# A two-layer decoder trunk on one core: latent attention driven by one list of steps, with stacked rotary queries, and FFN transposes moved into the next unit

## The chip, the cores and the metric

The kernel runs on one core of one Trainium2 chip. The metric is the device time of one execution, in microseconds, and what is compared is the median of several runs. An execution is a little longer than the span of its profile, which goes from the first to the last instruction.

The engines go by the names of the profile: PE is TensorE's matmuls and PEld its weight loads, DVE is VectorE, ACT is ScalarE, POOL is GpSimd, SP is SyncE, which issues the DMAs.

## The reference

The input is 256 tokens of width 1024 in float32. Two layers follow each other. Each layer has four sublayers, and behind each stands a layer norm of `ALPHA * x + delta`:

- a first FFN, half of `silu(x Wgate) * (x Wup)` times `Wout`, with an inner width of 2816;
- a mixer: forgetting attention (16 heads of 64) in layer 0, latent attention in layer 1;
- a second FFN of the same form;
- a projection of the layer's own input embedding, times a sigmoid gate of `x`.

The mixer that the change touches is the latent attention. From the stream that leaves layer 0 come, once, a compressed key/value of 256 columns (with an RMS norm) and one rotary key of 64 columns that all heads share. From the stream in layer 1 come compressed queries of 384 columns (with an RMS norm), and from these, per head, a query part of 128 columns without position and one of 64 columns that is rotated by position. The score of head h is

```
s = (q_nope . k_nope + rope(q_rope) . k_rope) / sqrt(192),   causal, then softmax
o = softmax(s) V,   V of 128 columns per head;   mix = concat(o) W_o
```

with 16 heads, and the rotation is `rope(x) = [x1 cos - x2 sin, x2 cos + x1 sin]` on the two halves of the 64 columns.

## The kernel before

**Precision by parts.** Every float32 operand of a matmul is kept as two parts: a high part, which a copy on ScalarE rounds to the format that TensorE takes at full rate, and a low part, the difference, which VectorE subtracts. A product is then three matmuls, high by high, high by low and low by high (`mm3`, L481). `parts` (L496) makes the two parts of something that TensorE has left in PSUM; weights are split the same way when they have landed (`Stream.split`, L149: the copy is L169, the subtraction L170).

**Tiles.** Tokens lie in two row blocks of 128. PSUM has eight banks, which are handed out from three rings (`bank`, L413): `y` with four, `h` with two, `tr` with two.

**The FFN** (`ffn`, L581) goes through eleven column chunks. The first two are computed with tokens as rows (`H`), so that their gated products must be transposed (`T`, L639, four transposes of 128 by 128). The other nine are computed transposed at once (`HT`, L651: 4 weight units of 24 matmuls, 256 columns wide), in three groups of three; the ring of a unit is `h` or `tr` by the chunk's number. Behind each group come the output products (`W`, L672, 512 columns wide). `T(0)` stands ahead of the first group and `T(1)` ahead of the second; ahead of the third stand the transposes of the compressed key/value, of the layer's input, or four idle ones. `ple_project` (L753) multiplies the layer's input behind the third group and takes four banks from `h`.

**The latent attention** (`mla`, L1217) is written out by hand. `dq` gives the compressed queries of one row block and normalizes them, `V` the values of four heads, `q_rope` the rotary queries of all 16 heads for one row block, `rope` (L1274) their rotation for eight heads: three multiplications and an addition, the addition of the first eight heads on GpSimd, the rest on VectorE. `transposed` turns the rotated queries, two heads to a transpose, and makes their two parts. Then the heads run through a pipeline: `gen(h + 1)` makes a head's keys and queries, `T(h - 1)` transposes the softmax weights of the head before, `QK(h)` makes the scores, `softmax(h)` (L1326) takes the row maxima (VectorE), the exponentials with their sums (ScalarE), the reciprocal (VectorE) and the division (GpSimd, L1344), `O(h - 2)` multiplies a finished head by its rows of the output weights, `AV(h - 1)` multiplies weights by values. `QK` (L1310) makes twelve matmuls a head: three for the part without position, three for the rotary part, each for a query block of 128 keys and one of 256. The rotary key of a pair of heads is kept twice, with zeros in the other head's half.

**What sets the order.** Each engine takes its instructions in the order in which the program issues them. Weights are loaded by SP into three raw buffers and split into ten slots (and a few lent tiles). When a split is issued is decided by a planner in `Stream`: it keeps estimates of when each engine is done, and `pump` (L242), called behind every `mm3`, splits the next unit if it has landed and the engines are free enough by the estimate. `hold` switches the pump off. `fill(n)` (L135) splits until n units are ready ahead, whatever the estimate. `ahead` (L128) issues only the high half, and `later` (L144) the low half. A unit that isn't ready when it is used is split at that point.

Of the kernel before, what the change touches and what calls it, by code (L numbers as in the profile page):

```python
# [30 lines left out]
LATE = 6  # L31
HAT = 12
FINE = 4
HOLD_MLA = True
AHEAD = {0: 4, 1: 4, 2: 4, 8: 4, 10: 4}
# [5 lines left out]
SW_DQ = 3  # L41
# [9 lines left out]
VT = {5: (2, (1,)), 8: (3, (0,)), 10: (3, (1,))}  # L51
# [345 lines left out]
class Trunk:  # L397
# [183 lines left out]
    def ffn(self, li, which, lni, kv=False, ple=False, at=None, cold=False):  # L581
# [57 lines left out]
        def T(c, ring="tr"):  # L639
# [59 lines left out]
        T(0)  # L699
        n = NCH  # L700
        late = [0, 2, 3, 4, 1] + list(range(5, n - STAG))
        for i, group in enumerate(GROUPS):
            if i == 1:
                T(1, "h")
            if i == 2:
                if kv:
                    self.kv_transpose()
                elif ple:
                    self.ple_transpose()
                else:  # L710
                    spare = self.bank("tr")
                    for k in range(4):
                        self.transpose(spare[:, 128 * k : 128 * k + 128], self.ident)
# [29 lines left out]
    def ple_transpose(self):  # L743
        nc = self.nc
        pt = self.ple_p
        tr = self.bank("tr")
# [6 lines left out]
    def ple_project(self, li):  # L753
# [3 lines left out]
        for t in range(2):  # L757
            for n in range(2):
                ps = self.bank("h")
# [434 lines left out]
    def kv_transpose_rope(self):  # L1194
# [3 lines left out]
        self.kr = [kvt[:, 1024 + 512 * s : 1536 + 512 * s].rearrange("p (i c) -> p i c", i=2) for s in range(2)]  # L1198
        b = self.bank("h")
        for t in range(2):  # L1200
            self.transpose(b[:, 128 * t : 128 * t + 128], self.kvtok[:, t, 256:384])
        nc.gpsimd.memset(self.kr[0][64:128, :, :].bitcast(F32), 0.0)
        nc.gpsimd.memset(self.kr[1][0:64, :, :].bitcast(F32), 0.0)
        for s in range(2):
            r = slice(64 * s, 64 * s + 64)
            self.parts(self.kr[s][r, 0, :], self.kr[s][r, 1, :], b[r, 0:256])

    def kv_transpose(self):
        b = self.bank("tr")
# [7 lines left out]
    def mla(self, li):  # L1217
# [9 lines left out]
        tmps = self.own([128, 4, 512], F32, "otb")  # L1227
        qk = self.own([128, 2, 2, 512], F32R, "qk")

        def dq(t, at=None, what=None, sweeps=SW_DQ):  # L1230
            ps = self.bank("y")
            self.moving(ps[:, 0:QR], t, ("dq",), QR, at, what, sweeps)
            rs = self.rms_scale(ps[:, 0:QR], QR, cqtok[:, t, 384:768])
            nc.vector.scalar_tensor_tensor(
                cqtok[:, t, 0:QR], ps[:, 0:QR], rs, qn, op0=ALU.mult, op1=ALU.mult
            )

        def V(g, ts, ring="h"):
            for t in ts:
                w = self.use(("kvv", g))  # L1240
                ps = self.bank(ring)
                for k in range(2):
                    self.mm3(
                        ps, lambda i: self.ckv[:, i, 256 * k + 128 * t : 256 * k + 128 * t + 128],
                        lambda i: w[:, i, 512 * k : 512 * k + 512], k == 0, k == 1,
                    )
                o = self.tl([128, 2, 512], F32R, "g4", 5)
                self.parts(o[:, 0, :], o[:, 1, :], ps)
                v[t, g] = o
# [11 lines left out]
        def q_rope(t, at=None, what=None):  # L1261
            ps = [self.bank("y") for _ in range(2)]
            for k in range(3):
                if k == at:
                    what()
                w = self.use(("qr", k))
                for n in range(2):
                    self.mm3(
                        ps[n], lambda i: cqt[:, i, k, 128 * t : 128 * t + 128],
# [152 lines left out]
        for h in range(16):  # L1422
            if 1 <= h < 15:
                gen(h + 1)
# [118 lines left out]
```

## Time and profile before

| | us |
|---|---|
| median of 3 runs | 1095.27 |
| range of the runs | 1094.84 to 1095.33 |
| profiled execution, its own time | 1094.83 |
| its span | 1092.7 |
| TensorE busy (matmuls) | 1075.1 |
| VectorE busy | 711.6 |
| ScalarE busy | 540.7 |
| GpSimd busy | 77.7 |

The profile is of one execution. Its table of groups gives, for each source line, engine and operation, the tile written and the tiles read, the count, the busy time, the mean of one in ns, and the idle time of the engine just before, with what ended it. The chain is followed back from the last instruction to what released it, so that it tells which work set the end. In a timeline, times are microseconds from the start of the span, and a row can hold several like instructions (x6). Matmuls are pipelined: the duration of one is longer than its distance to the next, so rates are read from a row that holds many. Line numbers are those of the listing above; most matmuls have L489, the helper, and all transposes but a few L493.

The latent attention lies between about 718 and 868 us of the span. In the stretch before it is the first FFN of layer 1, behind it the second.

### The profile page before, as it was taken

Reading aid. Unit: us, or ns where it says so; the run is one execution under the profiler, and the core shown is the slowest. Engines: PE = TensorE matmul, PEld = TensorE weight load, DVE = VectorE, ACT = ScalarE, POOL = GpSimd, SP = SyncE. Lnnn points to the kernel's source line nnn. Section 1 sums busy time; section 2 is a strip of 40 time slices with the busy share of each in tenths; the row PEclk is TensorE's granted clock in tenths of the full one; section 3 lists DMA queues with packets and bytes.
Section 4 is the critical chain, followed back from the end, with each engine's and each line's share of the span. In section 5 each row is a group of like instructions: output and inputs, shape, how many; then the busy total and the mean of one; then the engine's idle time right before and its main releaser. Section 6 shows DMA issues by size and latency. Waiting matters only on the chain.

```text
span 1092.7 us, 17699 instructions
## 1 busy us (share of the span) xinstructions
PE 1075.1 (98%) x7186; PEld 977.3 (89%) x7186; DVE 711.6 (65%) x1013; ACT 540.7 (49%) x796; POOL 77.7 (7%) x128
## 2 busy tenths in 40 slices
PE   9999999999999999999999999999999899999997
PEld 6999999899889999988899999988999789898986
DVE  5665545888897545548965554498776886455566
ACT  5554433667646434444554443245655465444431
POOL 0000000222200000001320000011111000000000
PEclk9999999999999999999999999999999999999999
DMA  8886652653358756455578554344453668565502
GB/s 283 287 276 241 192 185 81 193 173 134 120 169 294 231 185 198 148 182 164 168 256 270 189 183 159 97 103 132 145 160 116 191 221 295 182 201 193 179 15 77
DMA packets 150820, 198.54 MB, mean 182 GB/s; under 512 B 11858, under 2 KB 129874, under 8 KB 150740
## 3 DMA queue, kind: packets, MB, share of 16 engines
q1 hardware_dynamic: 150740, 197.43, 55.8%
q8 instruction: 56, 0.92, 0.3%
q14 instruction: 24, 0.20, 0.0%
HBM read 196.35 MB, written 1.05 MB: 181 GB/s over the span
## 4 chain that ended last, share of the span: by engine, by line
PE 83%; DVE 9%; issue 3%; ACT 2%; POOL 1%; DMA 1%; DVEq 0%; ACTq 0%; POOLq 0%; SPq 0%
PE h L489 35%; PE y L489 28%; PE tr L489 18%; DVE hl L170 2%; PE tr L493 2%; DVE x L569 1%; DVE st L551 1%; DVE x L550 1%; ACT hl L169 1%; POOL rs L561 1%; DMA raw<-in_ffn_w_in_dram 1%; ACT P L1337 1%; PE y L467 0%; DVE tr L1333 0%; DVE PT L499 0%
## 5 line engine op out<-in xcount | busy, mean ns | idle before, releaser
L170 DVE TENSOR_TENSOR hl<-raw,hl 128x1024 fp32r<-128x1024 f32 (+3 forms) x287 | 333.1, 1180 | 164.2 <-ACT hl L169 162.8
L169 ACT ACTIVATE hl<-raw 128x1024 fp32r<-128x1024 f32 (+3 forms) x287 | 285.3, 1016 | 193.3 <-PE y L489 94.0
L489 PE MATMUL h<-xT,hl 128*128 128x256 f32 x2064 | 245.5, 279 | 0.1
L489 PEld LDWEIGHTS h<-xT,hl 128*128 128x128 f32 x2064 | 240.9, 188 | 1.3 <-DVE qk L499 0.3
L489 PE MATMUL y<-hl,g 128*128 128x512 f32 x780 | 180.9, 390 | 0.0
L489 PEld LDWEIGHTS y<-hl,g 128*128 128x128 f32 x780 | 145.7, 188 | 29.8
L489 PE MATMUL tr<-xT,hl 128*128 128x256 f32 x864 | 102.7, 278 | 0.0
L489 PEld LDWEIGHTS tr<-xT,hl 128*128 128x128 f32 x864 | 100.8, 188 | 0.0
L489 PE MATMUL h<-hl,xT 128*128 128x512 f32 (+2 forms) x396 | 91.6, 381 | 0.7 <-DVE xT L499 0.6
L489 PEld LDWEIGHTS h<-hl,xT 128*128 128x128 f32 x396 | 70.8, 188 | 15.9 <-DVE xT L499 1.2
L489 PE MATMUL y<-hl,xT 128*128 128x512 f32 (+3 forms) x360 | 65.0, 334 | 0.2 <-DVE xT L499 0.2
L489 PEld LDWEIGHTS y<-hl,xT 128*128 128x128 f32 x360 | 55.4, 188 | 6.6 <-DVE xT L499 0.8
L561 POOL TENSOR_TENSOR rs<-ve,mhalf 128x1 f32<-128x1 f32 x16 | 15.2, 950 | 526.8 <-DVE ve L560 526.8
L498 ACT ACTIVATE xT<-tr 128x512 fp32r<-128x512 f32 x34 | 19.2, 596 | 55.7 <-PE tr L493 55.7
L499 DVE TENSOR_TENSOR g<-P,g 128x512 fp32r<-128x512 f32 x36 | 24.9, 693 | 25.1 <-ACT g L498 25.1
L498 ACT ACTIVATE g<-P 128x512 fp32r<-128x512 f32 x36 | 22.8, 632 | 31.0 <-DVE P L666 31.0
L489 PE MATMUL y<-hl,ota 128*128 128x512 f32 x144 | 36.0, 393 | 0.0
L170 DVE TENSOR_TENSOR otb<-raw,otb 128x1024 fp32r<-128x1024 f32 (+1 forms) x20 | 24.0, 1202 | 14.4 <-ACT otb L169 14.4
L170 DVE TENSOR_TENSOR qk<-raw,qk 128x1024 fp32r<-128x1024 f32 x21 | 25.7, 1223 | 11.7 <-ACT qk L169 11.6
L489 PEld LDWEIGHTS y<-hl,ota 128*128 128x128 f32 x144 | 26.0, 188 | 4.9
L665 ACT ACTIVATE P<-h 128x512 f32<-128x512 f32 x20 | 12.0, 598 | 37.1 <-PE h L489 37.1
L499 DVE TENSOR_TENSOR xT<-tr,xT 128x512 fp32r<-128x512 f32 x34 | 22.1, 682 | 12.2 <-ACT xT L498 12.2
(241 smaller groups left out, 1391.4 us busy)
## 6 DMA issues: line engine op xcount, KB each, us to landing
raw<-in_ffn_w_in_dram SPq DMA_DIRECT2D x172, 512.0 KB, 5.0
raw<-in_ffn_w_out_dram SPq DMA_DIRECT2D x44, 1024.0 KB, 5.2
raw<-in_fox_w_in_dram SPq DMA_DIRECT2D x11, 1024.0 KB, 5.3
raw<-in_ple_w_gate_dram SPq DMA_DIRECT2D x8, 1024.0 KB, 5.1
raw<-in_mla_w_o_dram SPq DMA_DIRECT2D x8, 1024.0 KB, 4.9
gb<-in_ln_g_dram SPq DMA_DIRECT2D x8, 512.0 KB, 6.4
gb<-in_ln_b_dram SPq DMA_DIRECT2D x8, 512.0 KB, 7.5
raw<-in_fox_w_o_dram SPq DMA_DIRECT2D x4, 1024.0 KB, 4.9
```

What stands on the lines that cost most here:

```text
L169: nc.scalar.activation(hi[:, c], src[:, c], AF.Copy)
L170: nc.vector.tensor_tensor(lo[:, c], src[:, c], hi[:, c].bitcast(F32), op=ALU.subtract)
L489: self.nc.tensor.matmul(out, lhsT, rhs, start=start, stop=stop)
L493: self.nc.tensor.transpose(out, in_, self.ident)
L498: self.nc.scalar.activation(hi, src, AF.Copy)
L499: self.nc.vector.tensor_tensor(lo, src, hi.bitcast(F32), op=ALU.subtract)
L550: nc.vector.scalar_tensor_tensor(xs, xs, alpha, y, op0=ALU.mult, op1=ALU.add)
L551: nc.vector.bn_stats(st, xs)
L561: nc.gpsimd.tensor_tensor(rs, ve, self.mhalf, op=ALU.pow)
L569: nc.vector.scalar_tensor_tensor(xs, xs, rs if i else mv[:, 0:1], self.gb[:, i, c0:c1], op0=ALU.mult if i else ALU.subtract, op1=ALU.add i ...
L665: nc.scalar.activation(gt, ps[0], AF.Silu)
L1337: nc.scalar.activation(P[:, c0:c1], b[:, c0:c1], AF.Exp, bias=nm[:, q : q + 1], scale=-1.0, accum_out=su[:, q : q + 1],)
```

## The change

- The rotary part of the scores is stacked. The 64 rotated columns of a head take 128 rows of one tile: their high parts one half, their low parts the other. One matmul against the key's high part (the same in both halves) gives high by high and low by high; a second against the key's low part, with zeros under the queries' low half, gives high by low. A head has ten score matmuls.
- For heads 0 to 7 the parts are made behind the transpose (`zT_first`: two copies and two subtractions on half the rows each). For heads 8 to 15 they are made ahead of it, side by side (`z_split`), and transposed together, one transpose a head and row block (`zT_last`).
- The rotation of heads 8 to 15 is a copy on ScalarE and four operations on GpSimd, and the subtraction for their low parts is on GpSimd as well. The addition of heads 0 to 7 is on GpSimd for row block 0 and on VectorE for row block 1.
- The division is on VectorE, and is a step of its own. Both row maxima stand ahead of both exponentials.
- A value tile's high copy and low subtraction are steps of their own, and so are the norm's scale, the reciprocal norm and the pump's fills.
- All steps of the latent attention stand in one list, `ORDER`, which a loop runs. Both row blocks of the compressed queries take the same order of terms.
- In the FFN each of the three transposes stands behind the first weight unit of its group, with the rings exchanged; `ple_project` alternates between `h` and `tr`.

```diff
+ORDER = (
+    "dq 0 0", "dq 0 1", "dq 0 2", "dq 0 3", "dq 0 4", "dq 0 5", "f 2", "dq 0 6", "hold 1", "dq 0 7", "dq 0 8",
+    "dq 0 9", "dq 0 10", "dq 0 11", "rms 0", "V 0 0", "V 0 1", "XT 1 0", "dqs 0", "vlo 0 0", "vlo 0 1", "V 1 0",
+    "l", "XT 1 1", "f 3", "dq 1 0", "dq 1 1", "dq 1 2", "dq 1 3", "cqT 0", "dq 1 4", "f 3", "dq 1 5", "dq 1 6",
+    "dq 1 7", "dq 1 8", "dq 1 9", "dq 1 10", "dq 1 11", "qr 0 0", "rms 1", "dqs 1", "rope 0 0 1", "vlo 1 0",
+    "V 1 1", "cqT 1", "exp", "qr 0 1", "qr 1 0", "f 3", "rope 1 0 0", "zT 0", "gen 0", "gen 1", "zT 1", "f 3",
+    "qr 1 1", "QK 0", "sm 0", "f 1", "QK 1", "sm 1", "div 1", "div 0", "f 3", "rope 0 1 2", "f 2", "vlo 1 1",
+    "V 2 0", "gen 2", "T 0", "gen 3", "f 1", "AV 0", "vlo 2 0", "rope 1 1 2", "a", "T 1", "f 4", "zs 0", "f 3",
+    "f 4", "QK 2", "zs 1", "y", "a", "sm 2", "div 2", "O 0 0", "O 0 1", "f 1", "AV 1", "f 4", "gen 4", "T 2",
...
+    "div 15", "l", "O 13 0", "AV 14", "f 1", "O 7 1", "gb", "hold 0", "O 8 1", "hold 1", "T 15", "O 9 1",
+    "AV 15", "O 14 0", "hold 0", "f 5", "f 3", "O 15 0", "ln 0", "O 10 1", "O 11 1", "O 12 1", "O 13 1",
+    "O 14 1", "XT 0 0", "XT 0 1", "O 15 1", "ln 1",
+)
...
-        def HT(c):
-            ring = "h" if c % 2 == 0 else "tr"
+        def HT(c, what=None):
+            ring = "tr" if c % 2 == 0 else "h"
             ps = [self.bank(ring) for _ in range(2)]
             for u in range(4):
+                if u == 1 and what:
+                    what()
...
-        T(0)
...
+        turns = (
+            lambda: T(0, "h"),
+            lambda: T(1, "tr"),
+            self.kv_transpose if kv else self.ple_transpose if ple else spare,
+        )
...
-                HT(c)
+                HT(c, turns[i] if c == group[0] else None)
...
-                ps = self.bank("h")
+                ps = self.bank(("h", "tr")[n])
...
-            self.parts(self.kr[s][r, 0, :], self.kr[s][r, 1, :], b[r, 0:256])
+            nc.vector.tensor_tensor(
+                self.kr[r, 1 + s, :], b[r, 0:256], self.kr[r, 0, :].bitcast(F32), op=ALU.subtract
+            )
...
+            if how == 2:
+                nc.scalar.activation(o, x, AF.Copy)
+                nc.gpsimd.tensor_tensor(tm[:, :, 0:32], o[:, :, 32:64], sn[0], op=ALU.mult)
+                nc.gpsimd.tensor_tensor(tm[:, :, 32:64], o[:, :, 0:32], sn[1], op=ALU.mult)
+                nc.gpsimd.tensor_tensor(o, o, cs, op=ALU.mult)
+            else:
...
+            (nc.gpsimd if how else nc.vector).tensor_tensor(o, o, tm, op=ALU.add)
...
+        def z_split(t):
+            z = zt[:, t, :].rearrange("p (h i d) -> p h i d", i=2, d=64)
+            nc.scalar.activation(z[:, :, 1, :].bitcast(F32R), z[:, :, 0, :], AF.Copy)
+            nc.gpsimd.tensor_tensor(z[:, :, 0, :], z[:, :, 0, :], z[:, :, 1, :], op=ALU.subtract)
...
-                self.mm3(
-                    b[:, c0:c1], lambda i: self.xT[:, q0 // 128, i, pair, :],
-                    lambda i: kr[:, i, 0:w], False, True,
-                )
+                for i in (0, 1 + (h % 2 if h < 8 else 1)):
+                    self.mm(b[:, c0:c1], zT[:, h, q0 : q0 + 128], kr[:, i, 0:w], False, i > 0)
...
+        def divide(h):
+            P, su = st[h]
             nc.vector.reciprocal(su[:, 0:2], su[:, 0:2])
-                nc.gpsimd.tensor_scalar(
-                    P[:, c0:c1], P[:, c0:c1], su[:, q : q + 1], 1.0, op0=ALU.mult, op1=ALU.mult
-                )
+            for q, (c0, c1) in enumerate(((0, 128), (128, 384))):
+                if DIV == "dve":
+                    nc.vector.tensor_scalar(P[:, c0:c1], P[:, c0:c1], su[:, q : q + 1], None, op0=ALU.mult)
...
+        for step in ORDER:
+            f, *x = step.split()
+            steps[f](*map(int, x))
```

In the list, `f n` is `fill(n)`, `a` is `ahead`, `l` is `later`, `dqs` the norm's scale, `cqT` the transposes of the compressed queries, `qr t n` the rotary queries of eight heads, `rope t n how` their rotation (`how` 2 is the one on GpSimd), `zT`, `zs` and `zU` are `zT_first`, `z_split` and `zT_last`, `vlo` a value tile's low part, `sm` the softmax without its division, `div` the division.

More of the change, by code (lines that the diff above doesn't have):

```diff
@@ L40 @@
 SW_KD = 0
-SW_DQ = 3
 SWEEPS = (
@@ L698, in ffn, with spare @@
         H(1, 1)
-        T(0)
         n = NCH
+        def spare():
+            tr = self.bank("h")
+            for k in range(4):
+                self.transpose(tr[:, 128 * k : 128 * k + 128], self.ident)
+        turns = (
[3 more added lines that the diff above has]
+        )
         late = [0, 2, 3, 4, 1] + list(range(5, n - STAG))
         for i, group in enumerate(GROUPS):
[L703 to L713, printed above, removed]
             for c in group:
@@ new lines, in dq, with rms @@
+        def dq(t, n):
+            if n == 0:
+                dqb[t] = self.bank("y")[:, 0:QR]
+            u, (i, j) = n % 4, ((0, 0), (1, 0), (0, 1))[n // 4]
+            w = self.use(("dq", u))
+            for kk in range(2):
+                self.mm(
+                    dqb[t], self.xT[:, t, i, 2 * u + kk, :], w[:, j, QR * kk : QR * kk + QR],
+                    n == 0 and kk == 0, n == 11 and kk == 1,
+                )
+            S.pump()
+        def rms(t):
+            dqr[t] = self.rms_scale(dqb[t], QR, cqtok[:, t, 384:768])
@@ new lines, in z_split, with zT_last @@
+        def z_split(t):
+            z = zt[:, t, :].rearrange("p (h i d) -> p h i d", i=2, d=64)
+            nc.scalar.activation(z[:, :, 1, :].bitcast(F32R), z[:, :, 0, :], AF.Copy)
+            nc.gpsimd.tensor_tensor(z[:, :, 0, :], z[:, :, 0, :], z[:, :, 1, :], op=ALU.subtract)
+            S.busy(act=512)
+        def zT_last(t, q, ring="tr"):
+            tr = self.bank(ring)
+            for i in range(4):
+                c = 512 * q + 128 * i
+                self.transpose(tr[:, 128 * i : 128 * i + 128], zt[:, t, c : c + 128])
+            h = 8 + 4 * q
+            nc.scalar.activation(
+                zT[:, h : h + 4, 128 * t : 128 * t + 128], tr.rearrange("p (k c) -> p k c", c=128), AF.Copy)
+            S.busy(act=512)
@@ L1362, in ot_of @@
                 return self.kvt[:, 512 * (h - 14) : 512 * (h - 13)].rearrange("p (i c) -> p i c", i=2)
-            h -= 6 if h >= 6 else 0
-            return OT[h // 4][:, h % 4]
+            return OT[h >= 10][:, (h + 2 * (h >= 10)) % 4]
         def AV(h):
-            if not OT:
-                OT.extend(self.own([128, 4, 2, 256], F32R, tag) for tag in ("ota", "otb"))
+            if h in (0, 10):
+                OT.append(self.own([128, 4, 2, 256], F32R, "ota" if h else "otb"))
             o = PT.pop(h)
@@ L1398, in mla @@
-        self.XT(1, (1,))
-        def last():
-            cq_transpose(0)
-            S.hold = True
-        dq(1, 16, last, 2)
-        S.hold = False
-        z = q_rope(0, 2, lambda: cq_transpose(1))
-        self.ready_for(AF.Exp)
-        for n in range(2):
-            rope(0, n, z[n])
-        z = q_rope(1)
-        for n in range(2):
-            rope(1, n, z[n])
-        self.transposed(0, zt[:, 0, :])
-        gen(0)
-        V(1, (1,), "y")
-        self.transposed(1, zt[:, 1, :], ring="y")
@@ new lines, in room, with hold @@
+        def room():
+            for t in range(2):
+                for n in range(2):
+                    y[t][n] = self.bank("y")
+        def hold(x):
+            S.hold = bool(x)
+        steps = dict(
+            dq=dq, rms=rms, dqs=dq_scale, cqT=cq_transpose, V=V, vlo=vlo, qr=q_rope, rope=rope, zT=zT_first,
+            zs=z_split, zU=zT_last, gen=gen, QK=QK, sm=softmax, div=divide, T=T, AV=AV, O=O, y=room, hold=hold,
+            f=S.fill, a=S.ahead, l=S.later, XT=lambda t, n: self.XT(t, (n,)),
+            exp=lambda: self.ready_for(AF.Exp), gb=lambda: self.load_gb(li, 1),
+            lend=lambda: S.lend("qk"), ln=lambda t: self.ln(t, y[t], ALPHA, LN_EPS),
+        )
```

182 lines of the change are left out of this document (70 added, 112 removed), and 12 rows, old and new, of the table ORDER.

## The prediction

> **What bounds the kernel now.** I read the page first: its span, its table of busy time and its chain.
>
> ```profile
> span 1092.7 us, 17699 instructions
> PE 1075.1 (98%) x7186; PEld 977.3 (89%) x7186; DVE 711.6 (65%) x1013; ACT 540.7 (49%) x796; POOL 77.7 (7%) x128
> PE 83%; DVE 9%; issue 3%; ACT 2%; POOL 1%; DMA 1%; DVEq 0%; ACTq 0%; POOLq 0%; SPq 0%
> ```
>
> TensorE is busy for 98% of the span and holds 83% of the chain, so what pays is TensorE work removed or a TensorE stall removed. Next I read the busy time of the latent-attention stage in three stretches (opening, heads, end), then who TensorE waited for in it.
>
> ```profile
> 718.00:761.20 43.20, 40.18 (x238) 34.64 (x236) 37.12 (x69) 23.29 (x44) 6.20 (x9) 1.00 0.47 136
> 761.20:845.60 84.40, 84.37 (x595) 78.85 (x596) 58.38 (x132) 50.90 (x119) 11.58 (x26) 1.00 0.44 135
> 845.60:868.00 22.40, 20.04 (x102) 16.09 (x101) 16.70 (x27) 10.11 (x18) 2.37 (x5) 1.00 0.63 203
> ```
> ```profile
> PE h L489 <- ACT PT L498: 1.7, 1, 1.7
> PE h L489 <- DVE PT L499: 1.2, 2, 1.0
> PE tr L493 <- DVE x L569: 1.2, 1, 1.2
> PE y L489 <- DVE ve L1166: 0.8, 1, 0.8
> ```
>
> The columns are the stretch, its length, then busy us of PE, PEld, DVE, ACT and POOL. TensorE stands still for 43.20 - 40.18 = 3.0 us in the opening, for nothing among the heads, and for 22.40 - 20.04 = 2.4 us at the end. In the opening VectorE is busy for 37.12 of 43.20 us: the stalls there are waits for low halves in a full VectorE queue, the largest (1.7 us) for head 0's transposed weights. Among the heads TensorE alone sets the pace, and VectorE has slack on paper (58.38 of 84.40).
>
> The chain in order of time gives the rates of TensorE.
>
> ```profile
> 54.75 11.31 PE h L489 x96
> 110.03 10.88 PE tr L489 x96
> 239.38 2.83 PE h L489 x24
> 356.81 11.31 PE h L489 x96
> 579.37 11.31 PE h L489 x96
> 690.65 11.31 PE h L489 x96
> 769.34 1.37 PE tr L489 x12
> 879.00 0.87 PE tr L493 x8
> 971.60 11.31 PE tr L489 x96
> ```
>
> A head's score matmuls (L1310) take 1.37 us for twelve: 0.114 us each, though six move 128 columns and six 256. Eight transposes take 0.87 us. An FFN unit of 96 matmuls runs at one of two rates, 11.31 or 10.88 us, and keeps it through a group of three: five of the twelve groups are slow (the five rows with 11.31, one of each), which costs 3 x 0.43 = 1.3 us a group.
>
> **The change part by part.** *Scores with stacked rope queries.* Per head two matmuls out of twelve go, one of 128 and one of 256 columns. All are on TensorE, on the path: 16 x 2 x 0.114 = -3.65 us. The Trainium skill (TensorE: Matmul & The Clock Gate, Back-to-back issue gap) gives about 81 ns for a sustained matmul of 128 columns; by that the sum would be 16 x (0.081 + 0.114) = 3.1 us; the row here makes no difference between the widths, so the row decides.
>
> *More transposes.* The rotated queries were transposed in 16 instructions; now heads 0 to 7 take 8, heads 8 to 15 take 16, both halves being stacked before the transpose. Eight more: +0.87 us.
>
> *Rotation of the last heads on GpSimd.* Off VectorE go two sets of these:
>
> ```profile
> L1284 DVE TENSOR_TENSOR ota<-y,rope 128x512 f32<-128x512 f32 x4 | 2.7, 678 | 0.0
> L1285 DVE TENSOR_TENSOR otb<-y,rope 128x256 f32<-128x256 f32 x4 | 1.6, 410 | 0.0
> L1287 DVE TENSOR_TENSOR ota<-ota,otb 128x512 f32<-128x512 f32 x2 | 1.4, 709 | 0.1
> L1287 POOL TENSOR_TENSOR ota<-ota,otb 128x512 f32<-128x512 f32 x2 | 2.6, 1296 | 9.4 <-DVE otb L1286 9.4
> L498 ACT ACTIVATE xT<-tr 128x512 fp32r<-128x512 f32 x34 | 19.2, 596 | 55.7 <-PE tr L493 55.7
> ```
>
> That is 2 x (0.678 + 2 x 0.410 + 0.709) = 4.4 us, less one addition of 0.71 us that comes back from GpSimd for row block 1: VectorE -3.7 us in its fullest stretch. GpSimd gets two sets of a product and an addition of 512 (1.30 us each) and two products of 256 (an estimate of half that, 0.65), and two subtractions of 1.30: 2 x 3.9 + 2.6 = 10.4 us. Their first reader is the transposes behind head 3, some 20 us later, so on the path they cost nothing; if GpSimd were that late, TensorE, which works in order, would stand. ScalarE gets eight operations of 0.6 us (two copies, two roundings, four evictions), 4.8 us beside 50.90 of 84.40.
>
> *Division on VectorE.* GpSimd's two multiplications per head become two of 128 and 256 columns in VectorE's queue. No such operation is in the trace; the nearest are two casts from SBUF to SBUF.
>
> ```profile
> L952 DVE CAST negc<-negc x1: 217/217/217, 225.3 to 225.3; 32x128 fp32r<-32x128 f32 x1
> L956 DVE CAST negc<-negc x1: 356/356/356, 225.5 to 225.5; 64x384 fp32r<-64x384 f32 x1
> DVE su L1342 <- ACT P L1337: 9.1, 13, 0.7
> DVE tr L1333 <- ACT P L1337: 7.6, 13, 0.6
> DVE hl L170 <- ACT hl L169: 7.0, 11, 0.7
> DVE qk L499 <- ACT qk L498: 1.6, 3, 0.6
> ```
>
> 0.217 us for 128 columns, and on the line to 0.356 for 384 about 0.287 for 256: 0.50 us a head. The upper bound is the two-source row, 0.410 for 256 and its half more for 128: 0.62; the lower is nothing, where it fills a wait of VectorE's own. I take 0.50. The last four rows are VectorE's waits among the heads (13 of them). Its queue is in order: behind the reciprocal, which waits for the exponentials, stand the low halves that TensorE needs. For 13 heads VectorE needs 58.38 + 9.1 + 7.6 + 13 x 0.50 = 81.6 us; TensorE needs 84.4 - 13 x 0.228 + 16 transposes (1.74) = 83.2. So it is just hidden, if the waits for ScalarE's high halves (7.0) are filled; the list puts the low half behind the division there. Both row maxima before both exponentials joins two waits into one and changes no length that I count. If the cover is gone, the excess is paid in full (a rival).
>
> *The list in the opening.* It defers the value tiles' low halves behind those that the next matmul needs, transposes the compressed queries after 8 of the second block's 24 matmuls (not 16), and takes VectorE work out; but the pump is held from the first projection on, fills put several splits of 1.2 us ahead of head 1's and 2's softmax, head 1 is divided before head 0, and head 0's transpose waits for that. What stood for head 0's weights after the transpose stands before it now. Bounds: all 3.0 us go, or VectorE's queue adds as much. Working the queue through with these durations, I come out near where it was: 0.
>
> *Projection of the layer input* (once a layer): it took both banks from the ring of the FFN unit just ended.
>
> ```profile
> 477.92 2.60 PEld L489 LDWEIGHTS h<-hl,g 128*128 128x128 f32 x12 [0.27 <-ACT P L665]
> 480.80 1.69 PEld L489 LDWEIGHTS h<-hl,g 128*128 128x128 f32 x8 [0.28 <-ACT ota L766]
> ```
>
> With banks of both rings neither wait is left: 2 x 0.55 = -1.1 us.
>
> *FFN transposes behind a first unit.* The same four transposes, no DMA; they move past 24 matmuls on TensorE, and their eviction past nothing on ScalarE and VectorE that is late. Readers come a group later, so the move itself costs 0; so does the rotary key's smaller split, one copy less on ScalarE. But a unit that follows 512-wide matmuls at once runs slow (0.118 us each, the row of 24), so up to 24 x 0.0045 = 0.11 us per group that was quick, and the transposes set the rate anew: five slow groups of twelve may become any number. I take 0, with two groups either way (2.6 us).
>
> *The end.*
>
> ```profile
> 861.00 1.23 DVE L170 TENSOR_TENSOR hl<-raw,hl 128x1024 fp32r<-128x1024 f32 x1 [0.77 <-ACT hl L169]
> 862.14 0.68 DVE L550 SCALAR_TENSOR_TENSOR x<-x,y 128x512 f32<-128x512 f32 x1
> 867.21 0.66 PE L493 MATMUL tr<-ident,x 128*128 128x128 f32 x4 [1.16 <-DVE x L569]
> ```
>
> The layer norm starts behind a weight split, and TensorE then waits 1.16 us for it. The list's fill of five, one step before, can put one more split (1.23 us) ahead of the norm: between 0 and +1.2, I take +0.6.
>
> Sum: -3.65 + 0.87 - 1.1 + 0 + 0 + 0.6 = -3.3 us. The profiled execution took 1094.83 us, 2.1 more than its span; the median of the runs is 1095.27. From the median: 1092.0.
>
> **The rivals.** *The opening is cured.* VectorE's 3.7 us less and the earlier transposes remove the 3.0 us and the 1.0 us for head 15's weights: 1092.0 - 4.0 = 1088.0. For it speaks that VectorE was 86% busy there; against it, that a full queue only moves its wait.
>
> *GpSimd holds VectorE.* Both read SBUF.
>
> ```profile
> L1044 POOL TENSOR_SCALAR P<-P,su x32: 371/478/1270, 230.7 to 291.0; 128x128 f32<-128x128 f32 x16, 128x256 f32<-128x256 f32 x16
> 845.34 0.83 POOL L1344 TENSOR_SCALAR P<-P,su 128x128 f32<-128x128 f32 x2 [4.77 <-DVE su L1342]
> 845.96 1.28 DVE L170 TENSOR_TENSOR hl<-raw,hl 128x1024 fp32r<-128x1024 f32 x1 [0.71 <-ACT hl L169]
> 853.94 1.22 DVE L170 TENSOR_TENSOR hl<-raw,hl 128x1024 fp32r<-128x1024 f32 x1
> ```
>
> GpSimd's operation of 0.37 us takes 1.27 when it meets a VectorE split; a split that starts 0.21 us before GpSimd's end takes 1.28 instead of 1.22. Ten new GpSimd operations, a split caught by every second for half an operation (0.65): 5 x 0.65 = 3.3 us in the full opening, so 1095.3, no gain. The Trainium skill (SBUF — State Buffer, Who interferes with whom) says that the second to issue blocks fully until the first has finished, for a VectorE operation with two SBUF inputs against one of GpSimd that reads SBUF. The first row agrees with it; the third shows 0.06 us where the rule would have 0.2.
>
> *VectorE becomes the bound among the heads: slower.* If its waits for ScalarE (7.0 and 1.6 us) are not filled, it needs 81.6 + 8.6 = 90.2 us against TensorE's 83.2: +7.0, so 1099.0. It decides once more than 1.6 of those 8.6 us are left. For it: the division stands in the queue that already waits for the exponentials. Against it: TensorE loses nothing in this stretch today.
>
> *The rate alone.* All groups quick: -6.5 (1085.5); all slow: +9.1 (1101). The trace shows no rule for the rate after transposes amid one unit.
>
> **How the numbers follow.** Forecast (1089.5 to 1093.5) 0.38; opening cured 0.24; GpSimd or the queue eats the gain 0.22; VectorE bound 0.11; rate alone 0.05, mostly upward. The range 1086 to 1098 takes in the cured opening with one and a half groups quicker, and the queue's case with two slower; about 0.2 is left out. A measurement of this kernel can tell about 0.2%, 2.2 us, from no change. Faster by more than that: forecast 0.35, cured 0.24, the rest 0.03: 0.62. Slower: VectorE bound 0.10, the others 0.05: 0.15. Within: 0.23.
>
> **What would show it.** Right: ten score matmuls a head in about 1.14 us; no wait between an FFN's last unit and the projection; TensorE idle in the opening near 3 us, now ahead of head 0's transposes; none among the heads; the layer norm's wait 1.2 to 2.4 us. Wrong: TensorE idle among the heads with VectorE as releaser (VectorE bound); less than 1 us idle in the opening (cured); VectorE splits over 1.3 us beside GpSimd's rotation (the lock); more or fewer than five groups at 11.31 (the rate).

## The result, and the profile after

The changed kernel took 1087.12 us (median of four runs, 1086.40 to 1088.67) beside 1095.24 us for the kernel before on the same chip: a ratio of 0.9931, with a 95% interval of 0.9918 to 0.9944, 8.1 us less. A later set of runs gave 0.9933 (0.9914 to 0.9951). The forecast was 1092.0: direction and range hold, but most of the gain came from a term that the prediction had set at 0. That the time lies within the range is in part luck.

First the page of the changed kernel: span and busy time.

```profile
span 1085.4 us, 17615 instructions
PE 1066.6 (98%) x7162; PEld 969.4 (89%) x7162; DVE 719.2 (66%) x1038; ACT 543.9 (50%) x803; POOL 74.5 (7%) x105
```

TensorE is still the bound, with 8.5 us less busy time. To find where the time went, both traces are cut where the transposes behind a sublayer's layer norm begin. Each row gives a stretch, its length, then the busy us of PE, PEld, DVE, ACT and POOL. Before, the rows are layer 0's two FFNs, layer 1's first FFN, the latent attention, and the last FFN:

```profile
0.00:190.60 190.60, 189.10 (x1254) 170.99 (x1255) 109.90 (x116) 92.23 (x109) 2.75 (x12) 1.00 0.68 221
318.94:498.61 179.67, 179.60 (x1227) 165.48 (x1226) 104.43 (x105) 86.39 (x99) 1.88 (x2) 1.00 0.60 197
537.30:716.76 179.46, 179.07 (x1229) 165.99 (x1228) 100.86 (x105) 80.53 (x95) 13.28 (x19) 1.00 0.59 191
716.76:878.83 162.07, 155.91 (x989) 139.11 (x988) 123.59 (x243) 89.44 (x185) 21.15 (x39) 1.00 0.46 141
878.83:1058.57 179.74, 179.67 (x1227) 165.49 (x1226) 105.13 (x106) 86.79 (x100) 1.88 (x2) 1.00 0.59 195
```

After, the same five:

```profile
0.00:190.14 190.14, 188.26 (x1254) 169.52 (x1255) 110.25 (x116) 92.28 (x109) 2.76 (x12) 1.00 0.67 222
318.56:496.67 178.11, 178.11 (x1227) 164.56 (x1226) 104.42 (x105) 86.19 (x99) 1.88 (x2) 1.00 0.59 198
535.36:712.48 177.12, 176.73 (x1229) 163.81 (x1228) 101.27 (x105) 80.41 (x94) 12.97 (x19) 1.00 0.60 193
712.48:873.13 160.65, 153.89 (x965) 136.95 (x964) 129.53 (x268) 92.90 (x193) 18.23 (x16) 1.00 0.47 143
873.13:1051.25 178.12, 178.12 (x1227) 164.56 (x1226) 106.14 (x107) 86.81 (x99) 1.88 (x2) 1.00 0.58 197
```

The four FFNs lost 0.46, 1.56, 2.34 and 1.62 us, 6.0 together; the attention lost 1.42; the rest of the span moved by 0.1. The instruction count of the FFNs is the same on both sides (x1254, x1227, x1229, x1227), so those 6.0 us are not work removed. The attention has 24 TensorE instructions fewer, and 2.02 us less TensorE work, but TensorE stands there for 6.76 us instead of 6.16.

The chain in order of time shows the FFN's rate: first a group whose transposes (x4) stand behind 24 matmuls, then the first unit of the next group, then the projection's first two banks and a head's scores.

```profile
32.26 2.74 PE tr L512 x24
34.99 0.44 PE h L516 x4
35.43 8.19 PE tr L512 x72
43.62 10.88 PE h L512 x96
...
87.15 2.83 PE h L512 x24
...
90.42 8.17 PE h L512 x72
...
476.42 1.38 PE h L512 x6
477.79 1.36 PE tr L512 x6
...
765.62 1.15 PE tr L512 x10
```

The 24 matmuls behind 512-wide ones take 0.118 us each (87.15), and right behind the four transposes the unit goes on at 0.1135 (8.17 for 72). Every full unit of the execution, 24 of 24, is at 10.88 or 10.89 us; none is at 11.31. The projection follows its FFN unit with no gap, and ten score matmuls take 1.15 us: both as forecast.

TensorE's waits in the attention, the four largest (us in total, times, longest):

```profile
PE tr L516 <- DVE P L1434: 1.8, 2, 1.4
PE h L512 <- DVE hl L193: 1.4, 2, 1.0
PE tr L516 <- ACT qk L521: 1.2, 1, 1.2
PE h L512 <- DVE PT L522: 0.9, 1, 0.9
```

The third row and 0.4 us of the first are head 0's transposes, waiting for the division; the other 1.4 us of the first are head 2's. (The third row names a copy on ScalarE, which ends at about the same time as the first half of the division. With head 0 divided first, below, the transposes start before that copy does, so the division is what they wait for.) The second row is head 4's query, waiting for low halves of weights. The fourth stands at the end (head 15's weights); a smaller one, 0.5 us, stands in head 0's output projection. The opening was not cured: the same view of its stretch adds up to 5.1 us, and to 2.9 us before.

### The profile page after: what moved, and what is told of

The parts are those of the page before. It is cut to its first block, busy times and chain, and to the rows that moved or that the text cites. A ratio compares the mean times of both kernels' runs of the same rounds, so it can differ in the third digit from the quotient of the medians.

```text
span 1085.4 us, 17615 instructions
## 1 busy us (share of the span) xinstructions
PE 1066.6 (98%) x7162; PEld 969.4 (89%) x7162; DVE 719.2 (66%) x1038; ACT 543.9 (50%) x803; POOL 74.5 (7%) x105
## 4 chain that ended last, share of the span: by engine, by line
PE 82%; DVE 9%; issue 3%; ACT 2%; DMA 2%; POOL 1%; SPq 1%; DVEq 0%; POOLq 0%; ACTq 0%
PE h L512 30%; PE y L512 28%; PE tr L512 22%; DVE hl L193 3%; PE tr L516 2%; DVE x L592 1%; DVE st L574 1%; DVE x L573 1%; ACT hl L192 1%; POOL rs L584 1%; DMA raw<-in_ffn_w_in_dram 1%; DMA raw<-in_mla_w_uq_dram 1%; SPq L345 0%; ACT P L1422 0%; DMA x<-in_x_dram 0%
## 5 line engine op out<-in xcount | busy, mean ns | idle before, releaser
L193 DVE TENSOR_TENSOR hl<-raw,hl 128x1024 fp32r<-128x1024 f32 (+3 forms) x275 | 320.6, 1184 | 158.5 <-ACT hl L192 157.5
L512 PE MATMUL tr<-xT,hl 128*128 128x256 f32 x1704 | 199.0, 277 | 0.0
L512 PEld LDWEIGHTS tr<-xT,hl 128*128 128x128 f32 x1704 | 196.3, 188 | 0.6
L512 PE MATMUL h<-xT,hl 128*128 128x256 f32 x1224 | 146.4, 278 | 0.4 <-DVE qk L522 0.4
L512 PEld LDWEIGHTS h<-xT,hl 128*128 128x128 f32 x1224 | 142.6, 188 | 1.8 <-DVE qk L522 0.6
L512 PE MATMUL y<-hl,otb 128*128 128x512 f32 x168 | 42.7, 397 | 0.7 <-DVE hl L193 0.5
L512 PEld LDWEIGHTS y<-hl,otb 128*128 128x128 f32 x168 | 30.3, 188 | 7.2 <-DVE hl L193 0.8
L193 DVE TENSOR_TENSOR qk<-raw,qk 128x1024 fp32r<-128x1024 f32 (+1 forms) x21 | 25.7, 1222 | 10.6 <-ACT qk L192 10.6
L192 ACT ACTIVATE otb<-raw 128x1024 fp32r<-128x1024 f32 (+1 forms) x20 | 20.8, 1040 | 19.1 <-PE y L512 10.8
L208 DVE TENSOR_TENSOR hl<-raw,hl 128x1024 fp32r<-128x1024 f32 (+1 forms) x24 | 28.9, 1205 | 1.4 <-ACT hl L204 1.3
```

The costliest lines, as they stand in the source:

```text
L192: nc.scalar.activation(hi[:, c], src[:, c], AF.Copy)
L193: nc.vector.tensor_tensor(lo[:, c], src[:, c], hi[:, c].bitcast(F32), op=ALU.subtract)
L208: nc.vector.tensor_tensor(lo, src, hi.bitcast(F32), op=ALU.subtract)
L512: self.nc.tensor.matmul(out, lhsT, rhs, start=start, stop=stop)
```

## Theories

*Rate:* transposes in the middle of a unit leave every FFN group at the quick rate, which gives some 5 us; the projection gives 1; the attention gives the rest, its removed matmuls being partly eaten by new waits of two kinds, the order of the two first divisions and GpSimd's rotation holding up VectorE's splits. *Chance:* any edit draws the rates anew, this draw was lucky, and the attention is what lasts.

## Experiments on the FFN

**The FFN's part alone**, on the kernel before.

```diff
-            ring = "h" if c % 2 == 0 else "tr"
+            ring = "tr" if c % 2 == 0 else "h"
...
+                if u == 1 and what:
+                    what()
```

> The kernel before with the FFN's part alone: the transposes of each group behind the 24 matmuls of its first unit, the two rings of the units exchanged. The projection of the layer input and the latent attention stay as before. Theory 'rate' (the transposes amid a unit leave every group at 10.88 us per 96 matmuls): all twelve groups quick, five times 1.3 us less and up to 0.11 us more for each first unit, so 4.9 us under the kernel before (in the traces before and after the four FFN stretches differ by 6.0 us, 1.1 of it the projection): 1090.3. Rival 'chance' (the rate of a group is drawn anew by any change, and the gain is the attention's): no fixed count of slow groups, most likely four to six, so within 2.6 us of the kernel before.

Measured: ratio 0.9952 (0.9935 to 0.9968), 4.5 us less on the medians; all twelve groups quick. The stretches of the two FFNs that end in the projection:

```profile
317.94:496.55 178.61, 178.40 (x1227) 164.47 (x1226) 104.47 (x105) 86.32 (x99) 1.88 (x2) 1.00 0.60 198
877.63:1056.26 178.63, 178.42 (x1227) 164.49 (x1226) 105.11 (x106) 86.58 (x100) 1.87 (x2) 1.00 0.59 196
```

Beside the changed kernel's 178.11 and 178.12 this leaves 0.5 us each for the projection. "Rate" holds.

**The FFN's part and the projection's banks undone**, on the changed kernel (the reverse of the diff above, and of the projection's).

> The changed kernel with the FFN's part and the projection's banks taken back; only the latent attention is changed. Theory 'rate': the attention is worth 1.4 us (the stretch between the layer norms fell from 162.07 to 160.65 us), slow groups come back (five, as before, if nothing ahead of them decides): 1093.8. Rival 'chance': the attention carries the gain of 8.1 us less the projection's 1.1, so 1088.2.

Measured: 0.9972 (0.9959 to 0.9984), by the ratio 3.1 us less than before, 2.4 us on the medians. "Chance" wanted 0.9935, "rate" 0.9987; the interval excludes the first widely and misses the second by a little; "rate" had counted on five slow groups. Three groups are slow again, two of them in layer 1's first FFN; the third is the first group of the FFN ahead of it, which begins

```profile
333.04 0.44 PE tr L516 x4
333.48 11.36 PE h L512 x96
```

They are three of the five slow groups of the kernel before. A fourth of the five, the first group of layer 0's first FFN, is quick here, though everything up to it is the same program.

**The projection alone**, on the kernel before.

```diff
-                ps = self.bank("h")
+                ps = self.bank(("h", "tr")[n])
```

> The kernel before with one word changed: the projection of the layer input alternates between the two rings of banks. The prediction's term: two projections, each without a wait of 0.55 us: 1.1 us less, 1094.1, and no wait between the last FFN unit and the projection. Rival: the banks only move the wait to the readers behind it, under 0.3 us.

Measured: 0.9999 (0.9986 to 1.0013), which can't tell 1.1 us from nothing. The chain shows that the edit alone does less than a third of what was expected: in the kernel before the last unit of the FFN lies in ring "h", so the first bank still waits, and only the second wait is gone. First the projection of the kernel before, then that of this one, whose 24 matmuls take 1.66 + 3 x 1.36 = 5.74 us, 0.15 less.

```profile
477.92 5.89 PE h L489 x24
```
```profile
476.15 0.61 ACT P L665
...
476.80 1.66 PE h L489 x6
478.46 1.36 PE tr L489 x6
```

The whole term needs the exchanged rings as well; it is what the FFN's part alone leaves over, 2 x 0.5 us. Three groups are slow in this execution, all of them among the five of before, and the first group of layer 0's first FFN is quick, though it is the same program as before: with transposes ahead of the unit the rate differs from execution to execution.

**Position or rings.** The change moved the transposes and exchanged the rings. Two kernels keep one of the two.

```diff
-                if u == 1 and what:
+                if u == 0 and what:
```

> The changed kernel with its exchanged rings, but each group's transposes ahead of the first unit, where they stood before the change. Theory 'position' (transposes amid a unit set the quick rate; transposes straight ahead of a unit leave the rate open): three to six of the twelve groups at 11.31 us per 96 matmuls, each 1.3 us, less up to 0.11 us for each first unit that no longer starts slow: 3 to 7 us slower than the changed kernel, whose ratio to the kernel before was 0.993. Rival 'rings' (the slow groups came from the unit's own bank, which the gate of the unit before still held): all twelve at 10.88 us, up to 1 us faster.

Measured: 0.9944 (0.9928 to 0.9960), 1.2 us behind the later set of the changed kernel, which the runs can't tell from nothing; the profiled execution, the slowest of the four (1093.75, the others 1088.58 to 1090.20), has four slow groups of twelve, one of which begins

```profile
332.68 0.44 PE h L516 x4
333.11 11.31 PE tr L512 x96
```

The other, with the transposes behind 24 matmuls and all rings as before:

```diff
-            ring = "tr" if c % 2 == 0 else "h"
+            ring = "h" if c % 2 == 0 else "tr"
...
-                ps = self.bank(("h", "tr")[n])
+                ps = self.bank(("tr", "h")[n])
```

> The changed kernel with the transposes behind the first 24 matmuls, but all rings of banks as before the change (units, transposes, the rotary key's and the layer input's exchanged back). Theory 'position': all twelve groups at 10.88 us, the first unit of the first group waits for the gate of the unit before it as it did before the change (0.3 to 0.5 us, four times): 0 to 2 us slower than the changed kernel. Rival 'rings': some groups at 11.31 us, 3 us slower or more.

Measured: 0.9941 (0.9928 to 0.9955), 0.9 us behind the same set, again not clear of noise, and all twelve groups quick, as at this place:

```profile
336.65 0.44 PE tr L516 x4
337.08 8.19 PE h L512 x72
```

So it is the position, by the rows of the profiles. The first kernel's expected cost (3 us or more) did not show in its four runs together. Its profile's four groups cost about 5 us; what sets that execution apart from the three faster ones is, by its size, a fall of the clock that took 3.4 us (last section), and how many slow groups those three had is not on record. Over all profiles of this study, 15 of 48 groups are slow with the transposes straight ahead of a unit (before 5, projection alone 3, FFN undone 3, transposes ahead 4), and 0 of 120 in the ten executions with the transposes behind 24 matmuls. The slow ones do not fall evenly: the first group of layer 0's second FFN and the third of layer 1's first are slow in all four of those executions, and six of the twelve places in none, so something besides chance bears on it, and what that is was not tested.

## Experiments on the attention

**A third rope matmul per segment put back.**

```diff
-                for i in (0, 1 + (h % 2 if h < 8 else 1)):
-                    self.mm(b[:, c0:c1], zT[:, h, q0 : q0 + 128], kr[:, i, 0:w], False, i > 0)
+                for i in range(3):
+                    self.mm(b[:, c0:c1], zT[:, h, q0 : q0 + 128], kr[:, i, 0:w], False, i == 2)
```

> The changed kernel with one rope matmul more for each segment of a head's scores (32 in all): the product of the two low halves, which the change leaves out; it is added, so the result is only finer. The prediction's term: 32 x 0.114 = 3.65 us more, 1090.8, twelve score matmuls in 1.37 us. Rival: the stretch of the attention lost 24 matmuls and only 2.0 us of TensorE work, so a score matmul is worth 0.08 us or less on the path: 2.7 us or less.

Measured: 0.9953 (0.9940 to 0.9967), 2.4 us more than the changed kernel's 0.9931, uncertain by 2. In the profiles the attention's stretch is 4.05 us longer (712.41 to 877.11), of which 1.7 is a fall of the clock (last section). A head's twelve take again

```profile
774.01 1.37 PE tr L512 x12
```

16 x (1.37 - 1.15) = 3.5 us of instructions, of which 0.6 us is regained in waits: the one of 1.2 us for head 0's transposes is 0.9 there, the one of 0.9 us for head 15's weights 0.6, since their releasers come little later. The size per matmul is the prediction's; on the path it is worth 2.4 to 3 us.

**Head 0 divided before head 1.** The changed kernel as it is went along as the control.

```diff
-    ..., "sm 1", "div 1", "div 0", "f 3", ...
+    ..., "sm 1", "div 0", "div 1", "f 3", ...
```

> The changed kernel as it is, beside the three below on one chip. Theory 'rate': twelve groups at 10.88 us again, since the transposes amid a unit decide it, and a ratio to the kernel before near 0.993. Rival 'chance': some groups at 11.31 in this execution. The stalls of the attention's opening stand where they stood: 1.2 and 0.4 us ahead of head 0's transposes, 1.4 us in head 4's query, 0.9 and 0.5 us elsewhere.

> The changed kernel with two steps of the list exchanged: head 0 is divided before head 1. Theory 'order': head 0's weights are ready 0.7 to 0.8 us earlier and out of the reach of GpSimd's first products, which stretched head 0's division from 0.64 to 1.39 us; TensorE's stand ahead of head 0's transposes (1.5 us) goes, everything behind moves up with it: 1.2 to 1.5 us less than the changed kernel. Rival 'lock decides': head 4's query waits for low halves that VectorE works off only when GpSimd's rotation is done; that moment stays, so the wait there grows by as much: under 0.4 us of gain.

Measured: control 0.9933 (0.9914 to 0.9951), twelve quick groups; head 0 first 0.9915 (0.9898 to 0.9932), 2.5 us less on the medians of the two. The intervals overlap; the profiles decide. The stretch of the attention up to its layer norm's transposes went from 149.68 us in the profile of the changed kernel to 148.20 (711.61 to 859.81), the 1.5 us forecast. The waits for head 0's transposes are gone, those for head 2 and head 4 stay:

```profile
PE tr L516 <- DVE P L1434: 1.4, 1, 1.4
PE h L512 <- DVE hl L193: 1.4, 2, 1.0
```

"Order" is right for head 0.

**The lock.** Three kernels ask what GpSimd's rotation costs. In the changed kernel VectorE's last two splits ahead of head 4's query take 3.73 us together:

```profile
757.55 1.22 DVE L208 TENSOR_TENSOR hl<-raw,hl 128x1024 fp32r<-128x1024 f32 x1
758.68 3.73 DVE L193 TENSOR_TENSOR hl<-raw,hl 128x512 fp32r<-128x512 f32 x2
```

GpSimd beside them, in the same kernel:

```profile
757.59 2.31 POOL L1335 TENSOR_TENSOR ota<-ota,rope 128x512 f32<-128x512 f32 x1
759.98 1.61 POOL L1340 TENSOR_TENSOR ota<-ota 128x512 f32<-128x512 f32 x1
```

The two take turns. GpSimd's product starts at 757.59, when the split of 757.55 runs; it takes 2.31 us instead of the 1.28 of the same product in the rotation before, and ends at 759.90. The two splits that VectorE begins at 758.68 are done only at 762.41; with GpSimd at rest the same two take 1.55 us (below). The Trainium skill (SBUF — State Buffer, Who interferes with whom) says that the one that issues second is blocked fully until the first has finished; these rows agree, 1.03 us for GpSimd and 2.2 us for the two splits. The prediction's third row, where an overlap of 0.2 us cost 0.06, does not fit it and stays unexplained.

The rotation of heads 8 to 15 on VectorE:

```diff
-    ..., "rope 0 1 2", ...  "rope 1 1 2", ...
+    ..., "rope 0 1 0", ...  "rope 1 1 0", ...
```

> The changed kernel with the rotation of the last heads on VectorE (8 operations, 0.69 + 2 x 0.41 + 0.69 us twice = 4.4 us more for VectorE, GpSimd 10 us less, ScalarE two copies less); the subtraction of the low halves stays on GpSimd. Theory 'lock': GpSimd's rotation costs VectorE 2.2 us on two splits (1.77 and 2.03 us instead of 0.69 and 0.95) and 0.75 us on head 0's division, so VectorE wins back 2.9 of the 4.4 us, and the end of the opening stays within 1.5 us: between 0.5 us faster and 1.5 us slower than the changed kernel, no operation on VectorE over its usual length by more than 0.3 us before the subtractions. Rival 'offload pays' (the prediction's 0 on the path, the lock only a detail): 3 to 4.4 us slower.

Measured: 0.9936 (0.9919 to 0.9953), the same as the control; the attention's stretch is 1.0 us longer than the changed kernel's (150.69). VectorE's 4.4 us of rotation take the place of 2.9 us of blocking, as "lock" has it (the 2.2 on the two splits, and 0.75 on head 0's division). But the subtractions, still on GpSimd, block the same splits once more, by 1.7 us:

```profile
758.99 1.85 DVE L208 TENSOR_TENSOR hl<-raw,hl 128x1024 fp32r<-128x1024 f32 x1
760.76 2.61 DVE L193 TENSOR_TENSOR hl<-raw,hl 128x512 fp32r<-128x512 f32 x2
```

The two splits are done at 763.37 instead of 762.41, most of the rest falling into time in which VectorE had waited (1.6 us between 752 and 755). So the move to GpSimd pays 1 us in the profile and nothing in the medians, not 3.7.

The second rotation and the subtractions later, ScalarE's copy along with them:

```diff
-    ..., "vlo 2 0", "rope 1 1 2", "a", "T 1", "f 4", "zs 0", "f 3",
-    "f 4", "QK 2", "zs 1", "y", "a", "sm 2", "div 2", "O 0 0", ...
+    ..., "vlo 2 0", "a", "T 1", "f 4", "f 3",
+    "f 4", "QK 2", "a", "sm 2", "div 2", "zs 0", "rope 1 1 2", "y", "O 0 0", ... "div 3", "zs 1", ...
```

> The list of the kernel with head 0 divided first, and GpSimd's second rotation and both subtractions moved behind head 2's division (the second rounding behind head 3's), so that GpSimd is at rest while VectorE works off the splits for head 4's query. Theory 'lock': those splits take 0.69 and 0.95 us again instead of 1.77 and 2.03, the wait of 1.4 us in head 4's query goes, and GpSimd meets other splits later, among the heads, where TensorE has them early: 1 to 1.5 us less than with head 0 first alone (whose ratio was 0.9915), 0.9905. Rival 'the lock only moves': the splits met later are late too: no gain or up to 2 us slower.

Measured: 0.9924 (0.9911 to 0.9938): between the changed kernel and head 0 first, not under it. The wait for head 4's query is gone, and a larger one stands elsewhere:

```profile
PE y L512 <- ACT ota L1332: 4.5, 1, 4.5
```

The copy frees the PSUM bank of the rotary queries. Moved behind head 2's exponentials, it keeps head 0's output projection waiting for that bank. The expectation had overlooked that reader.

The copy back in its place, only GpSimd's work late:

```diff
-                nc.gpsimd.tensor_tensor(tm[:, :, 0:32], o[:, :, 32:64], sn[0], op=ALU.mult)
...
+                def products():
...
+                if how == 3:
+                    rps[t, n] = products
```

The list has "rope 1 1 3" (the copy) where "rope 1 1 2" stood, "zs 0" and "rp 1 1" (the products) behind "div 2", "zs 1" behind "div 3".

> As late_rot, but ScalarE's copy of the second rotation's queries out of PSUM stays where the changed kernel has it, so that its bank comes free as early as there; only GpSimd's part (four operations) and both subtractions wait for head 2's division. In late_rot TensorE stood 4.5 us for that copy. Theory 'lock': with the copy back and GpSimd at rest beside the splits for head 4's query, these take 0.69 and 0.95 us, the wait of 1.4 us there goes and so does most of the 1.4 us ahead of head 2's transposes, whose maximum stands behind the splits: 1.4 to 2.1 us less than with head 0 first alone, ratio 0.990. Rival 'the lock only moves': GpSimd then meets the splits behind head 2's division and their readers stand instead: no gain or up to 2 us slower than head 0 first alone (0.9915 to 0.9935).

Measured: 0.9905 (0.9883 to 0.9928), median 1084.28 us (1083.78 to 1084.45), the lowest of all kernels here, though its interval does not part it from head 0 first alone. The attention's stretch is 147.11 us (712.29 to 859.40), 1.1 less than with head 0 first alone; 1.4 to 2.1 was forecast. The two splits take 1.55 us again:

```profile
757.02 1.55 DVE L193 TENSOR_TENSOR hl<-raw,hl 128x512 fp32r<-128x512 f32 x2
...
766.35 1.34 DVE L1444 TENSOR_SCALAR P<-P,su 128x128 f32<-128x128 f32 x2
```

The wait of head 4's query is gone, head 2's fell from 1.4 to 1.0, and a new one of 1.0 us stands ahead of a product with a head's weights:

```profile
PE h L512 <- DVE PT L522: 1.9, 2, 1.0
PE tr L516 <- DVE P L1444: 1.0, 1, 1.0
```

GpSimd's addition of 766.06 meets a division on VectorE in that stretch (1.34 us for the pair instead of 0.55). The lock costs, and part of it moves: both theories have some of it.

**The division back on GpSimd.**

```diff
-                    nc.vector.tensor_scalar(P[:, c0:c1], P[:, c0:c1], su[:, q : q + 1], None, op0=ALU.mult)
+                    nc.gpsimd.tensor_scalar(P[:, c0:c1], P[:, c0:c1], su[:, q : q + 1], 1.0, op0=ALU.mult, op1=ALU.mult)
```

> The changed kernel with the division back on GpSimd, at the same places of the list. VectorE loses 32 operations of 0.29 and 0.35 us (10.3 us in all). Theory 'VectorE has slack among the heads': nothing is won there; in the opening head 2's division stands behind the rotation and the subtractions in GpSimd's queue, so its transposes come later: 1 to 2.5 us slower than the changed kernel, or 1 us more if the lock meets VectorE's splits. Rival 'VectorE is the limit among the heads': 1 us faster or more.

Measured: 1.0003 (0.9990 to 1.0015), 7.7 us above the control's ratio: the sign of "VectorE has slack", at more than twice its size, and "VectorE is the limit" is refuted. The waits and the slow divisions:

```profile
PE tr L516 <- POOL P L1434: 5.4, 5, 1.6
```
```profile
800.28 2.66 POOL L1434 TENSOR_SCALAR P<-P,su 128x128 f32<-128x128 f32 x2 [5.06 <-ACT otb L521]
816.63 0.83 POOL L1434 TENSOR_SCALAR P<-P,su 128x128 f32<-128x128 f32 x2 [7.18 <-PE tr L516]
```

A head's two divisions take 0.83 us alone and 1.6 to 2.7 beside VectorE's splits, and in the new list the head's transposes follow closely. Attention and layer norm together are 8.9 us longer than the changed kernel's 160.65 (711.74 to 881.25); 3.4 of that is a fall of the clock (below), 5.5 the division. The expectation counted the opening alone; 2.7 of the 5.4 us are waited behind it.

## Why the prediction was right in direction, and where it was wrong

- **FFN transposes: the term that was mis-sized.** "I take 0, with two groups either way (2.6 us)". The first half of the step, that the transposes set the rate anew and that up to 0.11 us is paid for a first unit, is what the trace shows. The failed half is "may become any number": behind 24 matmuls of the same unit the rate is always the quick one. Five groups at 1.3 us less 12 x 0.11 give 5.2; the stretches gave 6.0 - 1.0 = 5.0. The prediction had named this case ("all groups quick: -6.5") and given it almost no chance, because no row of before showed transposes amid a unit. It had allowed for two groups either way; five came.
- **Projection, -1.1:** 2 x 0.5 us. Right.
- **Scores, -3.65:** 16 x 0.22 = 3.5 us of instructions, 0.11 us a matmul on the mean of the two widths, as the row of before had it; the two widths were not measured apart. On the path about 2.4 to 3, as some of it ends in a wait. The eight transposes more were not measured by themselves.
- **Opening, 0:** wrong by 2.2 us. TensorE's waits there grew from 2.9 to 5.1 us. The place was right (head 0's transposes, divided second: 1.5 us by experiment); head 4's query and head 2's transposes had not been foreseen. The prediction's premise, too, is only half right: it took the opening's stalls for waits for low halves, but its largest row, 1.7 us, names ScalarE's copy, the high half of head 0's weights. That copy stood behind head 1's exponentials, and these behind VectorE's maxima.
- **End, +0.6:** wrong sign. TensorE's waits for the layer norm's output fell from 2.0 to 0.3 us in the views of the two kernels, so the end repaid most of what the opening lost. The fill of five did not put one more split ahead of the norm; one fewer stands there. Before, three splits follow head 15's last subtraction, the third at 861.00, and the norm starts at 862.14 (the prediction's rows), 5.2 us behind the start of that subtraction. After, two follow it, and the norm starts 3.2 us behind it:

```profile
854.14 2.36 DVE L193 TENSOR_TENSOR hl<-raw,hl 128x1024 fp32r<-128x1024 f32 x2 [0.52 <-ACT hl L192]
856.41 0.68 DVE L573 SCALAR_TENSOR_TENSOR x<-x,y 128x512 f32<-128x512 f32 x1
```

- **Rotation on GpSimd, 0 on the path:** wrong. The rival's price, 3.3 us of blocked VectorE, is near the 2.9 measured, though by luck: it counted five splits held for half an operation, and it was two splits and a division. About 1.1 us of it reached TensorE (only GpSimd's work late, against head 0 first).
- **Division, 0.50 us a head, hidden:** the pair takes 0.55 us from start to end where nothing blocks it. Right in size. Hidden it is: between 766 and 842 us TensorE waits once, 0.3 us, and for a query. "VectorE becomes the bound" did not happen. What the prediction did not see is that the new list needs the division on VectorE.
- **Attention in sum:** -2.2 forecast, -1.4 measured. The forecast lies 4.9 us above the result: 5.0 too much for the FFN's rate, 0.8 too little for the attention, and the difference between single executions and medians. The rival with the cured opening (1088.0) lies close to the result, and its mechanism is refuted: the opening got worse.

## What to carry to other kernels

When a long stream of equal matmuls shows two rates, count them over several executions and move what stands at its start before assigning the rate to chance: four transposes inside the stream instead of ahead of it were worth more here than the 24 instructions taken off TensorE. Work that is moved to GpSimd is to be placed where VectorE does not run splits or divisions that somebody waits for, and its copy out of PSUM is to stay early, since the bank has readers too. Where a list decides the order, divide first what is read first.

## What the runs showed of the hardware

**Two rates.** The same 96 matmuls with their weight loads take 10.88 or 11.31 us (0.1133 or 0.1178 us each) at a granted clock of 1.00, and a group keeps its rate through 288 matmuls. The first unit of a second or third group, which stands behind 512-wide output products, begins at 0.118 (2.83 us for 24); that of a first group takes 2.74 to 2.83. Four transposes in its midst took it to 0.1135 in all 120 groups; transposes ahead of its first matmul left it open. What in TensorE holds the rate stays open; fewer than 24 matmuls ahead of the transposes were not tried.

**A fall of the clock behind the waits.** In eight of the fourteen profiled executions the granted clock falls once between 757 and 776, at the end of the attention's opening or right behind it. The control, and then the same window of the changed kernel's first profile, which has no fall; the clock is the third number from the end:

```profile
760.00:770.00 10.00, 7.56 (x33) 6.59 (x34) 7.54 (x19) 5.32 (x14) 4.24 (x3) 0.70 0.52 157
770.00:780.00 10.00, 10.00 (x67) 9.10 (x66) 6.02 (x15) 4.55 (x12) 0.00 (x0) 0.96 0.37 103
```
```profile
760.00:770.00 10.00, 7.14 (x45) 6.09 (x45) 7.90 (x20) 5.11 (x14) 4.78 (x3) 1.00 0.56 169
```

Cut finer, the fall is to half the clock, for 6.8 us here:

```profile
764.50:770.50 6.00, 6.00 (x21) 5.30 (x22) 4.22 (x12) 3.18 (x8) 0.00 (x0) 0.50 0.28 115
```

It costs (0.30 + 0.04) x 10 = 3.4 us here, and 1.7 or 3.4 us in each of the eight. The control's six runs bear it out as a reason why runs of one kernel spread: two with a mean granted clock of 0.998 took 1086.3 and 1086.5 us, the four with 0.995 or 0.996 took 1089.2 to 1089.9. It is also why the stretches above are compared between executions without a fall or with it taken off. The Trainium skill (TensorE: Matmul & The Clock Gate, HAM oscillation — how this bites in real kernels) puts the limit at gaps of more than about 3.4 us in which TensorE is idle; the longest wait in the control's opening is 1.4 us, so this fall came without such a gap. Of the eight executions only the one with the late copy has so long a wait (4.5 us). In the window of 760 to 770 us TensorE is busy for some 7 of 10 us in both executions, the one with the fall and the one without. In the 3.4 us ahead of each of the eight falls it was busy for at most 2.0 us, and in the kernel with only GpSimd's work late, which has no fall there, for at least 2.4 us in any 3.4 us between 744 and 774. But the other five without a fall there have a stretch of 3.4 us with 1.0 to 1.5 us of work, so a thin stretch alone does not decide; what does stays open.
